# Low-part score products of the neighbourhood stage: 64 rows each, an even and an odd head side by side

## The chip, the cores and the metric

The kernel runs on one core of one Trainium2 chip. The metric is the device time of one execution in microseconds (us); the time before is the median of three runs. TensorE (PE) multiplies, VectorE (DVE) and ScalarE (ACT) work on its results, GpSimd (POOL) does small elementwise work, SyncE (SP) issues the transfers.

## The reference

One layer of an encoder over two sequences of 2048 tokens with 1024 features each, in float32:

```
h = rms_norm(x); proj = h @ w_in          # q_a k_a v_a g_a | q_b k_b v_b g_b
o_a = windowed_gqa_sink(q_a, k_a, v_a, sink) * silu(g_a)     # 8 heads of 64, window +-128
o_b = neighbourhood_attn(q_b, k_b, v_b, rpb) * silu(g_b)     # 8 heads of 64
x = x + concat(o_a, o_b) @ w_out
y = x + (p @ w_ple) * sigmoid(x @ w_ple_gate)
```

The change is in `neighbourhood_attn`: the 2048 tokens are a grid of 32 rows of 64; each query sees 8 rows by 16 columns of keys around it, with a learned bias by relative position and a softmax over them. Heads have 64 features, so a score is a sum over 64 products.

## The kernel before, in words

The kernel has three stages on one core: first the projection and attention of group A (32 tiles of 128 tokens), then those of group B (64 units, from about 818 to 1845 us of the profile), then the output projections.

All products are made of float32 numbers split into a high part, rounded to a form that TensorE takes in one pass (fp32r), and a low part, the rest; a product of two numbers is high x high + high x low + low x high.

**Second stage.** A unit (`unit_b`, L808) is a block of 8 grid rows by 16 grid columns, thus 128 queries, and four of the eight heads; there are 2 halves of heads x 2 sequences x 16 blocks = 64 units. The keys that a block can see form a window of 12, 15 or 16 rows by 24 or 32 columns: n = 288, 360, 384 or 512 columns of scores (`window`, L30).

**How operands lie.** The 128 rows (partitions) of a score product hold two halves of 64. For an even head (e = 0) the tile `ks_b[0]` has the keys' high parts in rows 0 to 63 and their low parts in rows 64 to 127; for an odd head (e = 1) it is the other way round (`keys_b`, L710). The queries come in two tiles (`prep_b`, L791). `q1[e]` has the queries' high parts in both halves, so that one product of 128 rows gives high x high + high x low. `q2[e]` has the queries' low parts in the rows of the keys' high parts (0 to 63 for even heads, 64 to 127 for odd heads) and zeros in the other half, written once, ahead of the first stage (L456). So a head's scores are two products into one PSUM tile: the high product (by `q1`) starts the sum, the low product (by `q2`) ends it. In the profile they are the `scb` matmuls at L260, `scb<-ks_b,q1b` and `scb<-ks_b,q`.

**What follows a head's scores.** `softmax` (L272) adds the bias on DVE and takes the maximum in the same instruction, from PSUM to a tile `s` (L275). After the fourth head `exps` starts: the maxima are negated on DVE (L286), and ACT takes the exponentials of heads 0, 2, 1 and 3 (L291). Later come the transposes of the exponentials (`pt`, tile `ptb`), their split (L853, L854) and the products with the values (`po`, tile `pob`).

**What sets the order.** The tensor engine's instructions run in the order in which the program writes them: `mm` (L259) ties each to the one before it. That order is written by hand: each unit runs through `PLAN_B` (L94), whose entries give the part of the unit's time at which a step is put, and between the steps come the "fillers", the products of the projection of a later unit (tiles `pqk` and `pvg`, 512 columns each). The beginning of the plan is

```
PLAN_B = ((0.00, 1, "sc", 0), (0.03, 1, "sc", 1), (0.07, 1, "sc", 2), (0.09, 0, "po", 2),
          (0.11, 1, "sc", 3), (0.16, 0, "po", 3), (0.16, 1, "exp", 0), (0.24, 0, "fin", 0), ...
```

so that two fillers lie between heads 0 and 1, two between heads 1 and 2, and two (with the value products of the unit before, `po`, after the first) between heads 2 and 3.

**PSUM.** The score tiles (`scb`), the transposes (`ptb`) and `pgtb` share one set of three buffers, "sc" (L67, L68), taken in turn. A unit takes nine: heads 0 to 3, `pgtb` and four `ptb`. So head 3 takes the buffer that head 0 had, and its first product waits until head 0's softmax has read it.

The functions that the change touches:

Of the kernel before, what the change touches and what calls it, by code (L numbers as in the profile page):

```python
# [29 lines left out]
def window(b, cb):  # L30
    c0, nc_ = COL_WIN[cb]
    r0, wide, narrow = ROW_WIN[b]
    nr = wide if nc_ == 32 else narrow
    rows = 5 if nr == 15 else 4
    return r0, nr, c0, nc_, rows


def row_type(b):
    return (0, 1, 1, 2)[b]


def col_type(cb):
    return (0, 1, 1, 2)[cb]


def query_rows(b, cb, j):

    r0, _, _, _, rows = window(b, cb)
    k0 = r0 + rows * j
    see = [r for r in range(8) if k0 - 7 <= min(max(8 * b + r - 4, 0), 24) <= k0 + rows - 1]  # L50
    return (see[0], max(see[-1] + 1, 4)) if see[0] == 0 else (min(see[0], 4), see[-1] + 1)
# [49 lines left out]
def emit(ctx, tc, io):  # L101
# [5 lines left out]
    def ptile(shape, tag, name):  # L107
        tag = PSM.get(tag, tag)
        return pp.tile(shape, F32, tag=tag, name=name, bufs=PSB[tag])
# [135 lines left out]
    def pinned(ins):  # L245

        if last_pe:
            tc.add_manual_dep(ins.ins, last_pe.pop().name,
                              mybir.DependencyInfo(mybir.DependencyClass.NoSync, mybir.DependencyReason.DATA),
                              reason="tensor engine order")  # L250
        last_pe.append(ins.ins)
# [7 lines left out]
    def mm(out, lhsT, rhs, start, stop):  # L259
        pinned(nc.tensor.matmul(out, lhsT, rhs, start=start, stop=stop))  # L260
# [11 lines left out]
    def softmax(i, ps, n, bias, sm):  # L272

        s = main.tile([128, 512], F32, tag="s", name="s", bufs=SB)
        nc.vector.tensor_tensor_reduce(out=s[:, :n], in0=ps[:, :n], in1=bias, scale=1.0, scalar=-3.0e38,  # L275
                                       op0=ALU.add, op1=ALU.max, accum_out=sm["mx"][:, i:i + 1])
        sm["s"].append(s)

    def sm_tiles():
        return {"s": [], **{k: ap.tile([128, 4], F32, tag=k, name=k, bufs=3) for k in ("mx", "nm", "den", "rd")}}  # L280

    def exps(sm, n, fct, gs, sink=None):

        mx, nm, den, rd, ss = (sm[k] for k in ("mx", "nm", "den", "rd", "s"))
        if sink is None:
            nc.vector.tensor_scalar_mul(nm, mx, -1.0)  # L286
            yield
        else:
            nc.vector.scalar_tensor_tensor(out=nm, in0=mx, scalar=-1.0, in1=sink[1], op0=ALU.mult, op1=ALU.min)
        for n_, i in enumerate((0, 2, 1, 3) if sink is None else range(4)):  # L290
            ex = nc.scalar.activation(ss[i][:, :n], ss[i][:, :n], AF.Exp, bias=nm[:, i:i + 1],  # L291
                                      accum_out=den[:, i:i + 1])
            if sink is None and n_ == 0:
                P(ex)
        if sink is not None:
            es = ap.tile([128, 4], F32, tag="es", name="es", bufs=3)
            nc.vector.tensor_tensor(out=es, in0=sink[0], in1=nm, op=ALU.add)
            nc.scalar.activation(es, es, AF.Exp)
            yield
            nc.vector.tensor_tensor(out=den, in0=den, in1=es, op=ALU.add)  # L300
        nc.vector.reciprocal(out=rd, in_=den)
        nc.vector.tensor_scalar_mul(rd, rd, fct)
        g2 = ap.tile([128, 4, HD], F32, tag="g2", name="g2", bufs=2)
        nc.gpsimd.tensor_tensor(out=g2, in0=gs.rearrange("p (h d) -> p h d", h=4),
                                in1=rd.unsqueeze(2).broadcast_to([128, 4, HD]), op=ALU.mult)
        sm["g2"] = g2.rearrange("p h d -> p (h d)")
        yield
# [70 lines left out]
    def big(shape, dt, name):  # L378
        return ap.tile(shape, dt, tag="big", name=name, bufs=3)
# [3 lines left out]
    ps = ptile([128, 512], "ms", "pwarm")  # L383
# [78 lines left out]
    ks_b, w_b, held = [], {}, {}  # L462
# [345 lines left out]
    def unit_b(f):  # L808
        half, st = divmod(f - 2 * NT, 2 * NT)
        s, j = divmod(st, NT)  # L810
        b, cb = divmod(j, 4)
        _, gs = held[f]
        r0, nr, c0, ncol, rows = window(b, cb)
        kc, nch = rows * ncol, nr // rows
        n = nr * ncol
        if cb != 2:
            off, _ = BIAS_OFF[(row_type(b), col_type(cb))]
            if not bt:
                bt.append(big([128, 2, 4, 512], F32, "bias"))
            bt.append(bt[0][:, len(bt) % 2])  # L820
            nc.sync.dma_start(bt[-1][:, :, :n], io["bias"][half][:, off:off + 4 * n].rearrange("p (h n) -> p h n", h=4))
        bias = bt[-1]
        vw = [ap.tile([128, 4, 2 * HD], F32R, tag=("vp", "vr_")[j % 2], name="vw", bufs=3 - j % 2) for j in range(nch)]
        for j in range(nch):
            nc.sync.dma_start(vw[j][:kc].bitcast(F32).rearrange("p h d -> p (h d)"),
                              v_d[half, s, cb][r0 + rows * j:r0 + rows * j + rows]
                              .rearrange("r c h a d -> (r c) (h a d)"))

        sees = [query_rows(b, cb, j) for j in range(nch)]
        order = sorted(range(nch), key=lambda j: sees[j][1] - sees[j][0])  # L830
        at = [16 * sum(z - a for a, z in sees[:j]) for j in range(nch + 1)]
        sm, p_ts, got = sm_tiles(), [], {}

        def sc(h):
            ps = ptile([128, 512], "sc", "scb")
            for j, q in enumerate(qs[f]):
                mm(ps[:, :n].rearrange("p (r c) -> p r c", c=ncol), q[h % 2][:, 128 * (h // 2):128 * (h // 2) + 128],
                   ks_b[h % 2][:, r0:r0 + nr, h // 2, c0:c0 + ncol], j == 0, j == 1)
            softmax(h, ps, n, bias[:, h, :n], sm)
            if h == 3:  # L840
                got["ex"] = exps(sm, n, hr_b[:, st:st + 1], gs)
                next(got["ex"])

        def pt(x):
            h = (0, 2, 1, 3)[x]
            pt = ptile([128, 512], "pt", "ptb")
            for j in order:

                c = at[j] - 16 * sees[j][0]
                tr(pt[:kc, c:c + 128], sm["s"][h][:, kc * j:kc * j + kc], rowwise)  # L850
            p_t = main.tile([128, 2, 512], F32R, tag="p_t", name="p_t", bufs=3)
            hi, lo, pf = p_t[:kc, 0, :at[-1]], p_t[:kc, 1, :at[-1]], pt[:kc, :at[-1]]
            nc.scalar.copy(hi, pf)  # L853
            nc.vector.tensor_tensor(out=lo, in0=pf, in1=hi.bitcast(F32), op=ALU.subtract)  # L854
            p_ts.append(p_t)

        def po(x):
            h = (0, 2, 1, 3)[x]
            e, i = h % 2, h // 2
            if i == 0:  # L860
                got["po"] = ptile([128, 2, 256], "ms", "pob")
            if x == 0:
                got["ot"] = ap.tile([128, 2, 2, 128], F32, tag="ot", name="otb", bufs=2)
            po, ot = got["po"], got["ot"]
            for j in order[::-1]:
                a, z = sees[j]
                mm(po[:, i, :].rearrange("p (a q) -> p a q", a=2)[:, :, 16 * a:16 * z], vw[j][:kc, h, :],
                   p_ts[x][:kc, :, at[j]:at[j + 1]], j == order[-1], j == order[0])
            if i == 1:
                a, z = 64 * e, 64 - 64 * e  # L870
                pq = po.rearrange("p i (a q) -> p i a q", a=2)
                nc.scalar.copy(ot[a:a + 64], pq[z:z + 64])  # L872
                nc.vector.tensor_tensor(out=ot[a:a + 64], in0=pq[a:a + 64], in1=ot[a:a + 64], op=ALU.add)  # L873

        def fin(_):
            pgt = ptile([128, 2, 128], "sc", "pgtb")
            for i in range(2):
                tr(pgt[:, i, :], sm["g2"][:, 128 * i:128 * i + 128], rowwise)
            o_t = ap.tile([128, 2, 128], F32, tag="o_t", name="o_tb", bufs=2)
            nc.gpsimd.tensor_tensor(out=o_t, in0=got["ot"][:, :, 0], in1=got["ot"][:, :, 1], op=ALU.add)  # L880
            nc.vector.tensor_tensor(out=o_t, in0=pgt, in1=o_t, op=ALU.mult)
            nc.sync.dma_start(ob_d[s][b, :, 2 * half:2 * half + 2, cb, :], o_t)
        return {"sc": sc, "pt": pt, "po": po, "fin": fin, "prep": lambda _: nxt(f), "exp": lambda _: next(got["ex"])}


# [61 lines left out]
    qs = {}  # L947
# [105 lines left out]
    with tc.tile_pool(name="c", bufs=1, reuse_waits="tile") as op:  # L1053
# [190 lines left out]
        for m in range(7 * len(groups)):  # L1244
            n, i = divmod(m, 7)
# [92 lines left out]
```

## Time and profile before

| | |
|---|---|
| time, median of 3 runs | 2495.81 us (2495.41 to 2498.2) |
| the profiled execution | 2493.45 us; span from first to last instruction 2491.5 us |
| granted TensorE clock | 1.00 |
| second stage in the profile | from 818.1 us (first `scb` product) to about 1845 us |
| score products (`scb`) | 512 matmuls: 4 widths x 64 high and 64 low ones |

How to read the rows: the engine page gives busy time, its share of the span and the number of instructions. PE is the matmuls, PEld the loads of their stationary operand, which run beside them. A row of a group is line, engine, operation, out<-in, rows*columns of the stationary operand, shape and count, then busy us and the mean ns of one, then idle time of the engine ahead of it. In the timeline each row begins with the start in us and the length of what follows; neighbours of one kind are merged (x3). Matmuls overlap, so that one's length is longer than its distance to the next. A stretch row gives, for each engine, busy us and count, then the clock, the share of the DMA engines' time, and GB/s. A row of waits names who waited for whom, the sum in us, how often, and the longest.

### The profile page before, as it was taken

To read this page: it belongs to the slowest core of one execution; us is meant where nothing else is said; L and a number is where in the kernel's file an instruction comes from. 1 tells how busy PE (TensorE), PEld (TensorE's weight loads), DVE (VectorE), ACT (ScalarE), POOL (GpSimd) and SP (SyncE) were. 2 spreads that over 40 slices of the span, in tenths; PEclk is the share of its full clock that TensorE was granted. 3 is DMA by queue.
4 is the path that set the end of the run, shared out by engine and by line. 5 is a ranking of instruction groups with operands and counts; after the bars stand their busy time and mean duration, and the time that the engine had idled before them with its cause. 6 is when DMAs were issued, how large, how long until landed. Compare 5 with 4: busy or idle time off the path is not lost.

```text
span 2491.5 us, 39866 instructions
## 1 busy us (share of the span) xinstructions
PE 2470.3 (99%) x12920; PEld 2084.8 (84%) x12920; DVE 1733.7 (70%) x4274; ACT 1417.0 (57%) x3341; POOL 786.7 (32%) x1033
## 2 busy tenths in 40 slices
PE   9999999999999999999999999999999999999999
PEld 7888888888888888888888888888788888888887
DVE  7777777777775666666666676776547655687776
ACT  6677766767664566665566666665664222344443
POOL 4444444444434444444444443443110000000000
PEclk9999999999999999999999999999999999999999
DMA  6432233222254466556855566666977455756765
GB/s 207 140 111 97 82 94 100 90 92 94 90 183 139 145 196 183 166 181 189 272 184 182 184 208 197 199 204 217 302 245 279 155 172 176 265 172 219 243 226 169
DMA packets 246656, 438.86 MB, mean 176 GB/s; under 512 B 31920, under 2 KB 86320, under 8 KB 241200
## 3 DMA queue, kind: packets, MB, share of 16 engines
q1 hardware_dynamic: 246160, 436.30, 54.3%
q8 instruction: 103, 1.69, 0.3%
q14 instruction: 105, 0.86, 0.1%
q10 hardware_dynamic: 288, 0.01, 0.0%
HBM read 308.28 MB, written 133.19 MB: 177 GB/s over the span
## 4 chain that ended last, share of the span: by engine, by line
PE 93%; DMA 3%; DVE 2%; ACT 1%; issue 1%; POOL 0%; SPq 0%; DVEq 0%; ACTq 0%; POOLq 0%
PE pvg L260 14%; PE pqk L260 14%; PE acca L1161 13%; PE accc L1161 10%; PE pg L260 7%; PE pq L260 7%; PE scb L260 3%; PE ptb L263 3%; PE sc L260 3%; PE po L260 3%; PE pob L260 3%; PE pk L260 3%; PE pt L263 3%; PE pple L260 3%; DMA p<-p_t 1%; DMA stn<-x_n 1%
## 5 line engine op out<-in xcount | busy, mean ns | idle before, releaser
L291 ACT ACTIVATE s<-s,nm 128x384 f32<-128x384 f32 (+4 forms) x512 | 307.2, 601 | 328.4 <-DVE nm L286 199.5
L260 PE MATMUL pvg<-wb,xr 128*128 128x512 f32 x1536 | 461.4, 407 | 0.0
L260 PE MATMUL pqk<-wa,xr 128*128 128x512 f32 x1536 | 442.3, 410 | 0.0
L260 PEld LDWEIGHTS pqk<-wa,xr 128*128 128x128 f32 x1536 | 266.3, 189 | 37.0
L260 PEld LDWEIGHTS pvg<-wb,xr 128*128 128x128 f32 x1536 | 266.9, 189 | 31.7 <-DVE wb L157 0.8
L356 POOL TENSOR_TENSOR xr<-stx,xr 128x512 fp32r<-128x512 f32 x188 | 241.5, 1294 | 162.5 <-ACT xr L355 154.8
L1143 ACT CAST opd<-raw 128x512 fp32r<-128x512 f32 x224 | 131.5, 618 | 268.4 <-PE acca L1161 115.6
L1144 DVE TENSOR_TENSOR opd<-raw,opd 128x512 fp32r<-128x512 f32 x224 | 146.5, 686 | 143.8 <-ACT opd L1143 143.8
L260 PE MATMUL pg<-wb,xr 128*128 128x512 f32 x768 | 231.5, 409 | 1.0 <-DVE vv L506 1.0
L260 PE MATMUL pq<-wa,xr 128*128 128x512 f32 x768 | 220.5, 400 | 1.4 <-DVE wa L157 1.1
L275 DVE CUSTOM_DVE_ANT_0 s<-scb,bias 128x288 f32<-128x288 f32 (+3 forms) x256 | 141.8, 555 | 103.9 <-PE scb L260 99.0
L142 POOL TENSOR_TENSOR yb<-vrb,power 128x8 f32<-128x8 f32 x64 | 105.3, 1645 | 252.5 <-DVE vrb L747 244.2
L1161 PE MATMUL accc<-opd,wb 128*128 128x512 f32 x768 | 176.7, 389 | 0.0
L1161 PE MATMUL acca<-opd,wa 128*128 128x512 f32 x768 | 175.5, 389 | 0.0
L1161 PE MATMUL acca<-opd,s 128*128 128x512 f32 x768 | 175.4, 389 | 0.0
L1161 PEld LDWEIGHTS acca<-opd,wa 128*128 128x128 f32 x768 | 144.1, 188 | 29.9
L1161 PEld LDWEIGHTS acca<-opd,s 128*128 128x128 f32 x768 | 144.2, 188 | 29.9
L1161 PEld LDWEIGHTS accc<-opd,wb 128*128 128x128 f32 x768 | 144.1, 188 | 29.9
L873 DVE TENSOR_TENSOR otb<-pob,otb 64x512 f32<-64x512 f32 x128 | 88.2, 689 | 112.8 <-ACT otb L872 111.7
L260 PEld LDWEIGHTS pq<-wa,xr 128*128 128x128 f32 x768 | 139.2, 188 | 24.8 <-DVE wa L157 1.9
L260 PEld LDWEIGHTS pg<-wb,xr 128*128 128x128 f32 x768 | 137.1, 189 | 21.9 <-DVE vv L506 1.5
L260 PEld LDWEIGHTS pob<-p_t,vw 128*128 128x128 f32 (+2 forms) x832 | 132.0, 189 | 25.3 <-DVE p_t L854 5.3
(159 smaller groups left out, 5117.8 us busy)
## 6 DMA issues: line engine op xcount, KB each, us to landing
stx<-x_b SPq DMA_DIRECT2D x128, 256.0 KB
vw<-v_d SPq DMA_DIRECT2D x112, 256.0 KB
stx<-x_a SPq DMA_DIRECT2D x64, 256.0 KB
stn<-x_n SPq DMA_DIRECT2D x64, 256.0 KB
v_d<-vb SPq DMA_DIRECT2D x64, 256.0 KB
ple_d<-ev SPq DMA_DIRECT2D x64, 256.0 KB
xres<-x_r SPq DMA_DIRECT2D x64, 256.0 KB
x_d<-r SPq DMA_DIRECT2D x64, 256.0 KB
```

Of the source, the lines that this page charges most:

```text
L142: nc.gpsimd.tensor_tensor(out=y, in0=v, in1=power.broadcast_to([128, n]), op=ALU.pow)
L260: pinned(nc.tensor.matmul(out, lhsT, rhs, start=start, stop=stop))
L263: pinned(nc.tensor.transpose(out, in_, eye))
L275: nc.vector.tensor_tensor_reduce(out=s[:, :n], in0=ps[:, :n], in1=bias, scale=1.0, scalar=-3.0e38, op0=ALU.add, op1=ALU.max, accum_out=sm[ ...
L291: ex = nc.scalar.activation(ss[i][:, :n], ss[i][:, :n], AF.Exp, bias=nm[:, i:i + 1], accum_out=den[:, i:i + 1])
L356: low.tensor_tensor(out=lo, in0=raw, in1=hi.bitcast(F32), op=ALU.subtract)
L873: nc.vector.tensor_tensor(out=ot[a:a + 64], in0=pq[a:a + 64], in1=ot[a:a + 64], op=ALU.add)
L1143: P(nc.scalar.copy(hi, v))
L1144: P(nc.vector.tensor_tensor(out=lo, in0=v, in1=hi.bitcast(F32), op=ALU.subtract))
L1161: pinned(nc.tensor.matmul(ps, w[k][:, a, c:c + 128], o[:, b], start=i in (0, 1, 4) and k == 0 and j == 0, stop=k == 3 and j == 2, skip_gro ...
```

## The change

In `unit_b` the step `sc(h)` of an even head now issues only that head's high product. The step of the odd head issues its own high product, then the low products of both heads one behind the other, then both softmaxes. A low product names the 64 rows in which the queries' low parts lie (0 to 63 for the even, 64 to 127 for the odd head) in place of all 128; the rows that it no longer names hold zeros in `q2`. The plan, the tiles, the fillers and all else stay.

```diff
+        scores = {}
+
+        def score(h, j):
+            e, i = h % 2, h // 2
+            rows = slice(64 * e, 64 * e + 64) if j else slice(0, 128)
+            mm(scores[h][:, :n].rearrange("p (r c) -> p r c", c=ncol), qs[f][j][e][rows, 128 * i:128 * i + 128],
+               ks_b[e][rows, r0:r0 + nr, i, c0:c0 + ncol], j == 0, j == 1)
 
         def sc(h):
-            ps = ptile([128, 512], "sc", "scb")
-            for j, q in enumerate(qs[f]):
-                mm(ps[:, :n].rearrange("p (r c) -> p r c", c=ncol), q[h % 2][:, 128 * (h // 2):128 * (h // 2) + 128],
-                   ks_b[h % 2][:, r0:r0 + nr, h // 2, c0:c0 + ncol], j == 0, j == 1)
-            softmax(h, ps, n, bias[:, h, :n], sm)
+            scores[h] = ptile([128, 512], "sc", "scb")
+            score(h, 0)
+            if h % 2 == 0:
+                return
+            for g in (h - 1, h):
+                score(g, 1)
+            for g in (h - 1, h):
+                softmax(g, scores[g], n, bias[:, g, :n], sm)
             if h == 3:
                 got["ex"] = exps(sm, n, hr_b[:, st:st + 1], gs)
                 next(got["ex"])
```

## The prediction, made before the changed kernel ran

> **What bounds it now.** I read the top of the page first: busy time of each engine, then the chain of work that ended last.
>
> ```profile
> span 2491.5 us, 39866 instructions
> PE 2470.3 (99%) x12920; PEld 2084.8 (84%) x12920; DVE 1733.7 (70%) x4274; ACT 1417.0 (57%) x3341; POOL 786.7 (32%) x1033
> ...
> PE 93%; DMA 3%; DVE 2%; ACT 1%; issue 1%; POOL 0%; SPq 0%; DVEq 0%; ACTq 0%; POOLq 0%
> ```
>
> TensorE (PE) is busy for 99% of the span, and 93% of the chain is its matmuls. A share over the whole span can hide a stage, so I took the busy time by stretches for the second stage alone, from its first score product at 818.1 us on, and then the list of what PE waited for there.
>
> ```profile
> 818.10:1750.00 931.90, 930.18 (x5061) 779.85 (x5060) 632.29 (x1637) 571.55 (x1344) 406.91 (x430) 1.00 0.62 195
> 1750.00:1845.00 95.00, 89.47 (x498) 74.47 (x497) 55.86 (x142) 67.46 (x156) 12.48 (x23) 1.00 0.80 265
> ```
>
> ```profile
> PE ptb L263 <- ACT s L291: 3.4, 2, 2.9
> PE scb L260 <- DVE mx L275: 1.2, 1, 1.2
> ```
>
> Up to 1750 us PE stands still for 931.90 - 930.18 = 1.7 us of 931.9; DVE is busy for 632.29, ACT for 571.55, and the granted clock is 1.00. So in this stage time is what PE's instruction stream takes: a nanosecond taken out of the stream shortens the kernel, one put in lengthens it. No other engine is close to becoming the bound.
>
> **What the change takes out.** Which products are touched, and how many, stands in the groups with shapes kept apart: the low products (those that read tile q) of the four window widths.
>
> ```profile
> L260 PE MATMUL scb<-ks_b,q 128*128 128x512 f32 x64 | 25.6, 400 | 0.0
> ...
> L260 PE MATMUL scb<-ks_b,q 128*128 128x384 f32 x64 | 21.9, 342 | 0.0
> ...
> L260 PE MATMUL scb<-ks_b,q 128*128 128x360 f32 x64 | 20.8, 325 | 0.0
> ...
> L260 PE MATMUL scb<-ks_b,q 128*128 128x288 f32 x64 | 18.8, 294 | 0.0
> ```
>
> That is 4 x 64 = 256 low products, in 128 pairs (an even and an odd head), 32 pairs of each width. The mean of one (325 ns at 360 columns) isn't what it costs, as matmuls overlap: the cost is the distance from its start to the next one's start, in the timeline of PE.
>
> ```profile
> 1013.65 0.29 PE L260 MATMUL scb<-ks_b,q 128*128 128x288 f32 x1
> 1013.78 0.62 PE L260 MATMUL pvg<-wb,xr 128*128 128x512 f32 x2
> ```
>
> ```profile
> 1139.34 0.33 PE L260 MATMUL scb<-ks_b,q1b 128*128 128x360 f32 x1
> 1139.34 0.19 PEld L260 LDWEIGHTS scb<-ks_b,q 128*128 128x128 f32 x1
> 1139.50 0.33 PE L260 MATMUL scb<-ks_b,q 128*128 128x360 f32 x1
> 1139.50 0.35 PEld L260 LDWEIGHTS pvg<-wb,xr 128*128 128x128 f32 x2
> ...
> 1139.66 0.62 PE L260 MATMUL pvg<-wb,xr 128*128 128x512 f32 x2
> ...
> 1141.71 0.19 PEld L260 LDWEIGHTS pvg<-wb,xr 128*128 128x128 f32 x1
> 1141.77 0.45 PE L260 MATMUL pvg<-wb,xr 128*128 128x512 f32 x1
> 1141.82 0.19 PEld L260 LDWEIGHTS scb<-ks_b,q1b 128*128 128x128 f32 x1
> ```
>
> ```profile
> 1030.05 0.34 PE L260 MATMUL scb<-ks_b,q 128*128 128x384 f32 x1
> 1030.23 0.40 PE L260 MATMUL pvg<-wb,xr 128*128 128x512 f32 x1
> ...
> 1156.30 0.40 PE L260 MATMUL scb<-ks_b,q 128*128 128x512 f32 x1
> 1156.54 0.62 PE L260 MATMUL pvg<-wb,xr 128*128 128x512 f32 x2
> ```
>
> A low product holds the stream for 0.13, 0.16, 0.18 and 0.24 us at 288, 360, 384 and 512 columns, 0.71 us over the four widths. If the two of a pair ran wholly at once, one of them would vanish: 32 x 0.71 = 22.7 us, the most that the change can give. That each names 64 rows instead of 128 gives nothing by itself, as the products of the value stage with 96 and with 128 rows show, at the same 256 columns:
>
> ```profile
> L260 PE MATMUL pob<-p_t,vw 128*128 128x256 f32 x160 | 40.4, 285 | 0.1
> ...
> L260 PE MATMUL pob<-p_t,vw 96*128 96x256 f32 x96 | 22.3, 286 | 0.6 <-DVE p_t L854 0.6
> ```
>
> So the gain hangs on one thing that no row of this trace shows: that two products on the two halves of the rows overlap. I take it that they do, and ask how closely.
>
> **The weight loads.** Each product still has a load of 128 columns of its own. In the rows above a load begins when the product before it begins (1139.34 and 1139.34, 1139.50 and 1139.50), never sooner; where products are short, a product follows its load by 1141.77 - 1141.71 = 0.06 us, and the next load comes 1141.82 - 1141.71 = 0.11 us after the last. If the pair's second load waits like this for the pair's first product, the second product starts some 0.06 us behind the first, and a pair saves 0.13 - 0.06, 0.10, 0.12 and 0.18: 0.47 us over the widths, 32 x 0.47 = 15.0 us. If loads for different halves may run ahead, the second load is there 0.11 us after the first, thus mostly behind the high product ahead of the pair, and the gain is near 22.7 us. I take 15.0, the one that repeats what this trace shows, and keep 22.7 as the low end of the time. The Trainium skill, "TensorE: Matmul & The Clock Gate", section "Part 3: Packing small matmuls — row/col tiling", says that products on distinct row groups start about 4 ns apart and that a weight load may be pulled ahead of a running product if its row group differs; by it the sum would be 32 x (0.71 - 4 x 0.004), about 22.2 us, as an estimate. No run here shows it yet.
>
> **Switching between 128 and 64 rows.** Each pair has a product of 128 rows ahead and one behind, so 2 x 128 = 256 switches are added. This trace has none. The nearest rows are the changes between transposes, products of 120 rows and products of 128:
>
> ```profile
> 1201.93 0.49 PE L263 MATMUL ptb<-rowwise,s 128*120 128x128 f32 x3
> 1202.18 0.95 PE L260 MATMUL pqk<-wa,xr 128*128 128x512 f32 x3
> 1202.97 0.48 PE L260 MATMUL pob<-p_t,vw 120*128 120x256 f32 x3
> 1203.28 2.27 PE L260 MATMUL pqk<-wa,xr 128*128 128x512 f32 x9
> ```
>
> Three transposes take 0.25 us and three products of 120 rows 0.31 us, start to start; there is no room for a gap at the changes. So one end of the cost is nothing; below nothing is excluded, as a switch takes no work away. The other end is that a product waits until the one before has left the array: a product lasts 325 ns in the group row where the stream moves on after 160, so 0.165 us a switch, 256 x 0.165 = 42.2 us. I take nothing, the nearest row. A gap would eat the 15.0 us at 15.0 / 256 = 59 ns a switch, and the 22.7 us at 89 ns.
>
> **What moves.** The even head's softmax on DVE (L275) goes behind the odd head's products, and the even head holds its PSUM tile for longer. Head 3 takes the buffer that head 0 leaves, so the question is whether head 0's softmax is done in time.
>
> ```profile
> 1140.32 0.68 DVE L744 TENSOR_REDUCE ssqb<-sqb 128x8 f32<-128x512 f32 x1
> ...
> 1140.92 0.52 DVE L275 CUSTOM_DVE_ANT_0 s<-scb,bias 128x360 f32<-128x360 f32 x1
> ...
> 1142.05 0.33 PE L260 MATMUL scb<-ks_b,q1b 128*128 128x360 f32 x1
> ...
> 1143.15 0.19 DVE L286 TENSOR_SCALAR nm<-mx 128x4 f32<-128x4 f32 x1
> 1143.37 0.60 ACT L291 ACTIVATE s<-s,nm 128x360 f32<-128x360 f32 x1 [3.24 <-DVE nm L286]
> ...
> 1146.87 0.49 PE L263 MATMUL ptb<-rowwise,s 128*120 128x128 f32 x3
> ```
>
> The pair of heads 0 and 1 starts at about 1140.1 and is out at about 1140.5. With the reduction of L744 ahead of it on DVE, head 0's softmax ends at about 1140.8 + 0.6 = 1141.4. Head 3's first product, at 1142.05 before, comes about 0.25 us sooner (head 2's low product goes behind it, 0.16, and the first pair gives 0.1): 1141.8. That leaves 0.4 us, so I cost it at nothing. The maximum's negative (L286) comes behind two softmaxes instead of one, some 0.6 us later, and so do the exponentials on ACT, the casts of the next queries behind them and the reductions and scaling of DVE's queue. The transposes that read the first exponential start at 1146.87, and that exponential ends at 1143.37 + 0.60 = 1143.97: 2.9 us of cover. No transfer is moved, none is added, and no instruction goes or comes on SP's or POOL's queues.
>
> **Sum.** 2493.45 us (the profiled execution's own time; its span is 2491.5) - 15.0 + 0 = 2478.5. That execution lies 2.4 us under the median of 2495.81, so on the median's footing 2480.8. About 0.2% (5 us) is what a measurement of this kernel can tell from no change.
>
> **Rivals.** First, the switch has a price: the array empties before a product of the other row count may enter. By the upper end, with the loads finished inside the gap so that the pair overlaps fully, it is +42.2 - 22.7 = +19.5 us, 2515.3; it decides from 89 ns a switch. For it speaks that a product stays in the array for twice as long as the stream needs it; against it that transposes and 120-row products follow one another without a gap. The Trainium skill, "TensorEngine Tiling (Array Packing)", section "Key Properties", says that changing the tiling mode, not only the tile, drains the engine. This page speaks straight against the change; it gives no duration, so the bound is the row's. If the weight loads too can't be prefetched across the switch, add up to 0.06 us each, 256 x 0.06 = 15 us, 2531; I leave this tail out of the range.
>
> Second, the switch costs about half of that, 0.06 to 0.11 us: the time lies between 2488 (22.7 - 256 x 0.06 = 7.3 gained) and 2501 (5.5 lost), with no change in its middle.
>
> Third, the two products don't overlap although they lie side by side: 256 products of the same widths stay in the stream and nothing comes of it, 2495.8. Against it speaks only that they touch different rows and different PSUM tiles.
>
> Fourth, the pair overlaps but head 3 waits for head 0's softmax. It decides when DVE runs 0.4 us late at that place; with another 0.68 us instruction ahead it is 0.3 us a unit, 64 x 0.3 = 19 us, which eats the gain: 2500.
>
> **Chances.** Side by side without a gap: 0.47, forecast 2480.8, with 2473 (22.7 us) to 2487 as its own range (a lag of 0.11 us, the distance of two loads, in place of 0.06 gains 32 x 0.27 = 8.6). Full gap at the switch: 0.33. Half a gap: 0.12, of which a third each is faster, the same and slower. No overlap: 0.05. Late softmax: 0.03. Faster by over 0.2%: 0.47 + 0.04 = 0.51; within: 0.04 + 0.05 + 0.01 = 0.10; slower: 0.33 + 0.04 + 0.02 = 0.39. As both signs hold much, the range goes from the full gain to the full gap: 2473 to 2516.
>
> **What will show it.** Right, if in PE's timeline the second product of a pair starts at most 0.07 us behind the first, the next filler follows the first at a distance near 0.16 + 0.06 us at 360 columns, and the product ahead keeps its 0.16. The switch has a price if the distance from the high product to the pair, or from the pair to the filler, grows by 0.05 us or more beyond that. No overlap, if the two starts are 0.16 apart. The late softmax shows as PE waiting for DVE mx L275 at scb, 1.2 us in all now. I'm wrong above all if rows other than those of this trace set the price of a switch.

## The result, and the profile after

The changed kernel takes 2521.44 us (median of 4 runs, 2519.87 to 2522.72) against 2495.78 us before: a ratio of 1.0102, 95% interval 1.0089 to 1.0114. It is 25.7 us **slower**. The pairs do run side by side; the way into them and out of them costs more than that saves.

The head of the page of the changed kernel, and its chain:

```profile
span 2519.7 us, 39889 instructions
PE 2500.2 (99%) x12920; PEld 2063.3 (82%) x12920; DVE 1735.8 (69%) x4274; ACT 1416.3 (56%) x3341; POOL 788.7 (31%) x1033
...
PE 94%; DVE 2%; DMA 2%; ACT 1%; issue 1%; POOL 0%; SPq 0%; ACTq 0%; DVEq 0%; POOLq 0%
```

The span grew by 28.2 us, and PE's busy time by 2500.2 - 2470.3 = 29.9 us with the same 12920 matmuls. The engine is as "busy" as before, so this line can't show a gap: a matmul's row is longer than its stream (0.32 us against 0.16 at 360 columns), and a short wait between two matmuls is covered by the row ahead. The weight loads (PEld) went down by 21.5 us, mostly because the two loads of a pair now run at the same time (128 pairs x 0.18 us, about 23 us). The busy time by stretches, up to 1778 us (28 us later than the stretch of before), and what PE waited for:

```profile
818.10:1778.00 959.90, 957.95 (x5078) 759.88 (x5077) 638.59 (x1642) 573.40 (x1348) 408.03 (x430) 1.00 0.61 191
```

```profile
PE ptb L263 <- ACT s L291: 1.8, 1, 1.8
PE scb L260 <- DVE mx L275: 1.7, 2, 1.3
```

By these rows PE still stands still for only 2 us, and the wait for head 0's softmax (mx L275) is 1.7 us where it was 1.2: no other engine holds PE up. The whole loss lies in the second stage: from its first score product to its last product with the values it takes 1842.8 - 818.1 = 1024.7 us before and 1871.3 - 818.3 = 1053.0 us after, 28.3 more. In the groups of its products the low ones have become longer:

```profile
L260 PE MATMUL scb<-ks_b,q 64*128 64x512 f32 x64 | 16.1, 500 | 0.0
...
L260 PE MATMUL scb<-ks_b,q 64*128 64x384 f32 x64 | 14.3, 443 | 0.0
L260 PE MATMUL scb<-ks_b,q 64*128 64x360 f32 x64 | 13.7, 426 | 0.0
L260 PE MATMUL scb<-ks_b,q 64*128 64x288 f32 x64 | 12.7, 395 | 0.0
```

Busy time per group is about half of 64 times the mean (16.1 against 64 x 0.500 = 32.0): two rows always lie on top of each other. But the mean is 0.1 us more than before at every width (500 against 400, 395 against 294). Where it comes from is in the timeline. The first rows are PE before the change, at a low product of 360 columns; then come, after the change, PE around a pair of 360 columns, its loads, and PE around a pair of 512:

```profile
1139.50 0.33 PE L260 MATMUL scb<-ks_b,q 128*128 128x360 f32 x1
1139.66 0.62 PE L260 MATMUL pvg<-wb,xr 128*128 128x512 f32 x2
1140.12 0.33 PE L260 MATMUL scb<-ks_b,q1b 128*128 128x360 f32 x1
```

```profile
1148.97 0.32 PE L260 MATMUL scb<-ks_b,q1b 128*128 128x360 f32 x1
1149.22 0.43 PE L260 MATMUL scb<-ks_b,q 64*128 64x360 f32 x2
1149.58 0.73 PE L260 MATMUL pvg<-wb,xr 128*128 128x512 f32 x2
1150.15 0.33 PE L260 MATMUL scb<-ks_b,q1b 128*128 128x360 f32 x1
```

```profile
1148.74 0.19 PEld L260 LDWEIGHTS scb<-ks_b,q1b 128*128 128x128 f32 x1
1149.22 0.19 PEld L260 LDWEIGHTS scb<-ks_b,q 64*128 64x128 f32 x2 [0.29 <-issue]
1149.58 0.30 PEld L260 LDWEIGHTS pvg<-wb,xr 128*128 128x128 f32 x2 [0.17 <-issue]
```

```profile
1165.32 0.40 PE L260 MATMUL scb<-ks_b,q1b 128*128 128x512 f32 x1
1165.65 0.50 PE L260 MATMUL scb<-ks_b,q 64*128 64x512 f32 x2
1166.08 0.73 PE L260 MATMUL pvg<-wb,xr 128*128 128x512 f32 x2
1166.65 0.40 PE L260 MATMUL scb<-ks_b,q1b 128*128 128x512 f32 x1
```

Read the distances from start to start. The high product ahead of the pair used to hold the stream for 0.16 us at 360 columns; now the pair starts 0.25 us after it, **0.09 us late**. Its two loads start together, at 1149.22, at the very moment at which the pair's products are listed, and not 0.23 us ahead as the high product's load (1148.74 for 1148.97): so the products' listed start is not yet their stream, and the load stands in the open. The filler of 128 rows comes 0.36 us after the pair (0.16 of stream, 0.20 more), and its load too starts only with it, at 1149.58. The two fillers then take 0.57 us where two took 0.46 (1139.66 to 1140.12), as the first waits for that load. At 512 columns the three distances are 0.33, 0.43 and 0.57 us: 0.09, 0.19 and 0.11 more than one product's 0.24, one product's 0.24 and two fillers' 0.46. Both loads carry the mark "issue": PEld was idle although nothing that the profile shows held it. In the waits of the loads after the change this is the longest entry; before the change there was none with that mark.

```profile
PEld scb L260 <- issue: 38.8, 127, 0.4
```

From the starts of all 128 pairs: the distance from the high product to the pair is 91 ns over one product's length, at each of the four widths; from the pair's second product to the filler 193 ns over; from that filler to the next 106 ns over. That is 0.390 us a pair whatever its width, for which one product of 0.13 to 0.24 us is saved: a loss of 0.260, 0.230, 0.212 and 0.152 us at 288, 360, 384 and 512 columns, 32 x 0.854 = 27.3 us, against 28.2 in the span and 25.7 in the medians.

### The profile page after: what moved, and what is told of

Read it like the earlier page. It is cut to its first block, busy times and chain, and to the rows that moved or that the text cites. A ratio compares the mean times of both kernels' runs of the same rounds, so it can differ in the third digit from the quotient of the medians.

```text
span 2519.7 us, 39889 instructions
## 1 busy us (share of the span) xinstructions
PE 2500.2 (99%) x12920; PEld 2063.3 (82%) x12920; DVE 1735.8 (69%) x4274; ACT 1416.3 (56%) x3341; POOL 788.7 (31%) x1033
## 4 chain that ended last, share of the span: by engine, by line
PE 94%; DVE 2%; DMA 2%; ACT 1%; issue 1%; POOL 0%; SPq 0%; ACTq 0%; DVEq 0%; POOLq 0%
PE pvg L260 15%; PE pqk L260 14%; PE acca L1171 13%; PE accc L1171 10%; PE pg L260 7%; PE pq L260 7%; PE scb L260 4%; PE ptb L263 3%; PE pk L260 3%; PE sc L260 3%; PE pob L260 3%; PE po L260 3%; PE pple L260 3%; PE pt L263 3%; DMA stn<-x_n 1%
## 5 line engine op out<-in xcount | busy, mean ns | idle before, releaser
L260 PE MATMUL pvg<-wb,xr 128*128 128x512 f32 x1536 | 472.9, 415 | 0.4 <-DVE wb L157 0.4
L260 PEld LDWEIGHTS pvg<-wb,xr 128*128 128x128 f32 x1536 | 260.7, 189 | 53.7 <-issue 17.2
L275 DVE CUSTOM_DVE_ANT_0 s<-scb,bias 128x288 f32<-128x288 f32 (+3 forms) x256 | 136.7, 554 | 63.7 <-PE scb L260 63.1
L1171 PEld LDWEIGHTS acca<-opd,wa 128*128 128x128 f32 x768 | 144.2, 188 | 29.9
L1171 PEld LDWEIGHTS accc<-opd,wb 128*128 128x128 f32 x768 | 144.2, 188 | 29.9
L1171 PEld LDWEIGHTS acca<-opd,s 128*128 128x128 f32 x768 | 144.2, 188 | 29.9
```

The costliest lines, as they stand in the source:

```text
L1171: pinned(nc.tensor.matmul(ps, w[k][:, a, c:c + 128], o[:, b], start=i in (0, 1, 4) and k == 0 and j == 0, stop=k == 3 and j == 2, skip_gro ...
```

## The experiments

**Theory:** a change between products of 128 rows and of 64 costs about 0.195 us each way: the array empties (0.09 us), and then the weight load, which otherwise runs ahead under the product before, stands in the open (0.10 us). **Rivals:** the moved softmaxes and the longer held score tile; the overlap itself; any change of the number of rows.

### The order alone

The changed kernel with 128 rows named everywhere:

```diff
-            rows = slice(64 * e, 64 * e + 64) if j else slice(0, 128)
+            rows = slice(0, 128)
```

> The changed kernel's order of instructions on every engine, but the low products name all 128 rows again. Theory (a change between products of 128 and of 64 rows costs about 0.196 us, whatever else is moved): no switch is left and nothing overlaps, so the time is that of the kernel before, 2495.8 us within 3. Rival (the even head's late softmax and the longer held PSUM tile cost the time): it stays near the changed kernel's 2521 us.

Measured: 2495.39 us against 2494.67 of the kernel before beside it, ratio 1.0002 (0.9993 to 1.0011). The same order on every engine costs nothing that can be measured; what was moved is not the cause.

```profile
1139.43 0.33 PE L260 MATMUL scb<-ks_b,q1b 128*128 128x360 f32 x1
1139.59 0.49 PE L260 MATMUL scb<-ks_b,q 128*128 128x360 f32 x2
1139.91 0.62 PE L260 MATMUL pvg<-wb,xr 128*128 128x512 f32 x2
```

From the high product to the filler 0.48 us for three products, against 0.61 us (1148.97 to 1149.58) with the pair on 64 rows, which has one length less.

### The rows alone

The order of before, each low product on its 64 rows:

```diff
             for j, q in enumerate(qs[f]):
-                mm(ps[:, :n].rearrange("p (r c) -> p r c", c=ncol), q[h % 2][:, 128 * (h // 2):128 * (h // 2) + 128],
-                   ks_b[h % 2][:, r0:r0 + nr, h // 2, c0:c0 + ncol], j == 0, j == 1)
+                rows = slice(64 * (h % 2), 64 * (h % 2) + 64) if j else slice(0, 128)
+                mm(ps[:, :n].rearrange("p (r c) -> p r c", c=ncol), q[h % 2][rows, 128 * (h // 2):128 * (h // 2) + 128],
+                   ks_b[h % 2][rows, r0:r0 + nr, h // 2, c0:c0 + ncol], j == 0, j == 1)
```

> The order of the kernel before, with each low product naming its 64 rows, alone between products of 128 rows. Theory: 256 lone products give 512 switches, 512 x 0.196 = 100 us, and nothing overlaps: 2596 us. Rival (what costs is that two products run in the array at once and write two PSUM tiles): a lone product of 64 rows is free, 2496 us.

Measured: 2586.67 us, ratio 1.0369 (1.0353 to 1.0385), 92 us slower.

```profile
1168.17 0.33 PE L260 MATMUL scb<-ks_b,q1b 128*128 128x360 f32 x1
1168.42 0.43 PE L260 MATMUL scb<-ks_b,q 64*128 64x360 f32 x1
1168.78 0.73 PE L260 MATMUL pvg<-wb,xr 128*128 128x512 f32 x2
1169.35 0.32 PE L260 MATMUL scb<-ks_b,q1b 128*128 128x360 f32 x1
```

```profile
PEld scb L260 <- issue: 78.2, 254, 0.4
PEld pvg L260 <- issue: 34.5, 168, 0.3
```

A lone product of 64 rows has the very distances of the pair: 0.25, 0.36, 0.57 us. So the price doesn't come from two products in the array, and the loads' idle time called "issue" has doubled (it was 38.8 us, 127 times, at the pairs). The sum by distances is 256 x 0.388 = 99 us; some 7 us of it were given back, of which the waits of PE that the profile names give 4 (7.0 us in the stage before, 2.6 here), and the rest is open.

### Half of the pairs

Only heads 2 and 3 are paired:

```diff
-            if h % 2 == 0:
+            if h == 2:
                 return
-            for g in (h - 1, h):
+            for g in (h - 1, h) if h == 3 else (h,):
                 score(g, 1)
```

The diff leaves out two lines: heads 0 and 1 name 128 rows, and the softmaxes follow the same rule.

> Only heads 2 and 3 are paired with 64 rows; heads 0 and 1 run as before, with 128 rows. Half of the pairs: theory 64 x (0.392 - 0.178) = 13.7 us, 2509.5 us (12.8 by half of the measured loss). If the loss came from a delay that arises once a unit, with the second pair or with the first, it would be all of 25.7 us or nothing.

Measured: 2508.51 us, ratio 1.0055 (1.0041 to 1.0068), 13.8 us: half of the pairs, half of the loss.

### 96 rows in place of 64

In the order of before, the low products of the even heads name 96 rows, those of the odd heads 128. The product then uses `rows` as in the run with the rows alone:

```diff
+                rows = slice(0, 96) if j and h % 2 == 0 else slice(0, 128)
...
```

> The order of the kernel before; the low products of the even heads name 96 rows (0 to 95, of which 64 to 95 hold zeros), those of the odd heads 128. Theory (the price belongs to the change to a half of the rows): nothing, 2495.8 us within 3, as the value products of 96 and 120 rows stand among those of 128 without a gap. Rival (every change of the number of rows costs it): 128 products, 256 switches, 256 x 0.196 = 50 us, 2546 us.

Measured: 2496.28 us against 2494.67, ratio 1.0005 (0.9996 to 1.0014).

```profile
1138.25 0.33 PE L260 MATMUL scb<-ks_b,q1b 128*128 128x360 f32 x1
1138.41 0.33 PE L260 MATMUL scb<-ks_b,q 96*128 96x360 f32 x1
1138.58 0.63 PE L260 MATMUL pvg<-wb,xr 128*128 128x512 f32 x2
```

0.16 and 0.17 us, as with 128 rows. The price comes with 64 rows, and not with every number below 128. So the rows that I had taken as nearest, products of 120 rows among those of 128, were no test of it: 96 and 120 rows stand among 128 without a gap.

### Both products of a pair on the same half

```diff
-            e, i = h % 2, h // 2
+            e, i = 0 if j else h % 2, h // 2
```

> The changed kernel, but the odd head's low product reads the even head's operands, so that both products of a pair lie on rows 0 to 63 (the odd heads' low part is thus the even heads'). Theory (the overlap needs different halves; the switches stay): a second product's length comes back for each pair, 32 x 0.71 = 22.7 us on 2521.4, so 2544 us, and up to 14 us more if its load isn't made ahead. Rival (any two products of 64 rows overlap): 2521 us.

Measured: 2539.7 us, ratio 1.0179 (1.0163 to 1.0196), so 0.0077 more than the changed kernel, 19 us.

```profile
1154.33 0.32 PE L260 MATMUL scb<-ks_b,q1b 128*128 128x360 f32 x1
1154.59 0.59 PE L260 MATMUL scb<-ks_b,q 64*128 64x360 f32 x2
1155.11 0.73 PE L260 MATMUL pvg<-wb,xr 128*128 128x512 f32 x2
```

The pair's stretch is 1155.11 - 1154.59 = 0.52 us in place of 0.36: one stream more. The overlap comes from the different halves. Within one half the second load starts 0.108 us after the first, and the second product 0.27 us after the first one: the first product's load of 0.11 us and its stream of 0.16. The distances of all pairs give some 22.5 us; the 3 us between that and the measured 19 lie within the intervals.

### Each pair twice

The first issue of a pair doesn't end the sums (`last` is handed to the product's stop flag), the second does:

```diff
...
-            for g in (h - 1, h):
-                score(g, 1)
+            for last in (False, True):
+                for g in (h - 1, h):
+                    score(g, 1, last)
```

> The changed kernel with each pair of low products issued twice, one pair behind the other (the low part is thus added twice). It measures a product of 64 rows behind products of 64 rows. Theory (the price belongs to the change of rows alone, and within 64 rows loads are made ahead): one more product length per pair, 22.7 us, 2544 us. If loads aren't made ahead within 64 rows: 128 x 0.105 = 13.4 us more, 2558 us. Rival (each pair pays the whole price at both of its ends): 128 x 0.392 - the part that overlaps, 2571 us or more.

Measured: 2546.03 us, ratio 1.0206 (1.019 to 1.0222), 0.0104 above the changed kernel, 26 us with an uncertainty of some 5.

```profile
1154.73 0.32 PE L260 MATMUL scb<-ks_b,q1b 128*128 128x360 f32 x1
1154.98 0.60 PE L260 MATMUL scb<-ks_b,q 64*128 64x360 f32 x4
1155.51 0.73 PE L260 MATMUL pvg<-wb,xr 128*128 128x512 f32 x2
```

```profile
1154.98 0.30 PEld L260 LDWEIGHTS scb<-ks_b,q 64*128 64x128 f32 x4 [0.29 <-issue]
1155.51 0.30 PEld L260 LDWEIGHTS pvg<-wb,xr 128*128 128x128 f32 x2 [0.23 <-issue]
```

Four products from 1154.98 to 1155.51, 0.53 us against 0.36 for two: the second pair costs its stream and no more (22.6 us by all distances). Behind 64 rows, 64 rows are free of the price, and the second pair's loads run ahead again: the four loads lie within 0.30 us of 1154.98, and the second pair starts only at 1155.26. This run also splits the price. The second pair starts 105 ns beyond a stream's length after the first, which is the first pair's load in the open: its second loads too start 0.105 us after its first ones. The filler starts 87 ns beyond one stream after the second pair, a gap without a load in it. So one change is a gap of 0.09 us and a load of 0.105 us, in both directions. The two parts are measured; that the array empties in the 0.09 us is my reading, as no row shows the array itself.

### Two pairs behind one another, and the control

All four high products at the unit's beginning, then the four low ones; the fourth score tile comes from the projections' buffers, and the four softmaxes follow. The control names 128 rows. Lines and ends of lines left out are marked by dots:

```diff
-    (0.00, 1, "sc", 0), (0.03, 1, "sc", 1), (0.07, 1, "sc", 2), (0.09, 0, "po", 2), (0.11, 1, "sc", 3), ...
+    (0.00, 1, "sc", 0), (0.00, 1, "sc", 1), (0.00, 1, "sc", 2), (0.00, 1, "sc", 3), (0.09, 0, "po", 2), ...
...
-            if h % 2 == 0:
+            if h < 3:
                 return
-            for g in (h - 1, h):
+            for g in range(4):
                 score(g, 1)
...
```

> Control for the next run: the four high products of a unit at its beginning, then the four low products, all of 128 rows; the fourth score tile comes from the projections' buffers, and the softmaxes follow the group. No switch, nothing overlaps: 2496 us, a few us more if the four softmaxes in a row hold up the transposes or the score buffers.

> The same order as its control, with the low products on 64 rows: two pairs in a row, so two switches a unit in place of four. Theory (price per switch): 128 x 0.196 = 25.1 us paid, 22.7 us gained, 2.4 us over the control, thus about 2498 us. Rival (price per pair): 25.7 us over the control, about 2521 us.

Measured: the control 2499.16 us, ratio 1.0016 (1.0007 to 1.0025); with 64 rows 2503.55 us, ratio 1.0036 (1.0023 to 1.0049). The first of these is the timeline of the control, the second that of the 64 rows:

```profile
1139.52 0.82 PE L260 MATMUL scb<-ks_b,q1b 128*128 128x360 f32 x4
1140.17 0.81 PE L260 MATMUL scb<-ks_b,q 128*128 128x360 f32 x4
1140.82 1.31 PE L260 MATMUL pvg<-wb,xr 128*128 128x512 f32 x5
```

```profile
1141.57 0.82 PE L260 MATMUL scb<-ks_b,q1b 128*128 128x360 f32 x4
1142.32 0.60 PE L260 MATMUL scb<-ks_b,q 64*128 64x360 f32 x4
1142.85 0.73 PE L260 MATMUL pvg<-wb,xr 128*128 128x512 f32 x2
```

With half of the switches and the same overlap the loss shrinks from 25.7 us to 4.4 over the control (2.4 was expected, and the distances of all units give 2.4; the 2 us between lie within the intervals). The eight products take 1.28 us in place of 1.30, and the first filler behind them takes 0.11 us more (from the starts of all fillers), its load in the open. By these figures a unit should gain where two products are longer than 0.39 us: only at 512 columns, 2 x 0.237 = 0.474, so 16 units x 0.08 = 1.3 us as an estimate, less than a measurement can tell and less than what the grouping itself costs here. No version beat the kernel before.

## Why the prediction was wrong

**What bounds the kernel, and what a product costs:** right. The second stage follows PE's stream: the distances of the pairs account for 27.3 of the span's 28.2 us, and in the run with doubled pairs the second pair costs its stream.

**That the two halves overlap:** right, and more closely than forecast. I had taken a lag of 0.06 us from a load that waits for the product before; the second product starts 3 ns behind the first, as the two loads start together. So the full 22.7 us came out of the stream, the upper of my two values, before the switches took more. The Trainium skill, "TensorE: Matmul & The Clock Gate", section "Part 3: Packing small matmuls — row/col tiling", gave about 4 ns, and the trace agrees with 3.

**Switching between 128 and 64 rows:** this is the step that failed. "I take nothing, the nearest row": the transposes and the products of 120 rows have no gap, but neither has the run with 96 rows, while 64 rows have one even alone; so those rows were no change of this kind. The price is 0.195 us, 256 x 0.195 = 49.9 us against 22.7 gained; 89 ns was the point of decision. The first rival had the right mechanism; its upper end of 0.165 us was too high for the gap (0.09) and left the load out (0.105), which I put at up to 0.06 and outside the range. For a load in the open, the distance of two loads, 0.11 us in my own rows, was the figure to take, not the 0.06 from a load to its product. The time, 2521.4, lies between its 2515.3 and the 2531 of its tail, and above the range's 2516; that it came near 2515.3 is in part luck, as one term was too high and the other missing. The Trainium skill, "TensorEngine Tiling (Array Packing)", section "Key Properties", says that a change of the tiling mode drains the engine. The trace agrees so far as it shows a gap of 0.09 us at each change, and it shows a second cost, the load, that the section doesn't name. I had that rule in hand and gave it less weight than rows that didn't bear on it.

**What moves:** right. Order and softmaxes cost 1.0002 (0.9993 to 1.0011), and PE's wait for head 0's softmax was 1.7 us where it had been 1.2.

**No overlap, and the late softmax:** both rivals fall: no overlap by the pair's 3 ns and by the stream that the run on one half adds, the late softmax by the run of the order alone.

## What to carry to other kernels

Two products of 64 rows on different halves do run at once, but each excursion, the step from 128 rows to 64 and back, cost 0.39 us in this kernel, 1.6 to 3 times the product that a pair saves. Count excursions, not products: put as many half-row products behind one another as the PSUM tiles allow, and pair only if what is saved in one excursion is longer than 0.39 us (no run here reached a gain in that way). A price that no row shows has to be bounded by rows of the same kind of change; where there is none, its upper end belongs into the range with all its parts, the exposed load too.

## What the runs showed of the hardware that was not expected

- Two weight loads for different halves start together (3 to 4 ns apart). Among products of 128 rows, and among those of 64, a load runs ahead of its product, mostly by about one stream (0.16 us at 360 columns, 0.23 behind a filler); between 128 and 64 rows it doesn't in any pair (1 to 2 ns).
- The price is the same at 288 and at 512 columns, for a lone product and for a pair (0.25, 0.36 and 0.57 us at 360 columns in both).
- 96 rows beside 128 cost nothing (1.0005, 0.9996 to 1.0014), 64 rows beside 128 cost 0.195 us a change.
- The busy share of 99% stayed as it was with 27 us more of distances in the stream; the loads' idle time marked "issue" is where they show.
